# Banded attention by chunks of queries, two heads side by side on the array, and latent value products two key tiles at a time

## The chip, the cores and the metric

The kernel runs on one core of one Trainium2 chip. The metric is the device time of one execution in microseconds. The core has a matrix engine (TensorE; PE in the profile), a vector engine (VectorE, DVE), a scalar engine (ScalarE, ACT), a general engine (GpSimd, POOL) and a synchronisation engine (SyncE, SP), on whose queue nearly all transfers of this kernel are issued. Products go from SBUF into banks of PSUM, and VectorE and ScalarE read them there.

## What is computed

Two layers of a hybrid diffusion backbone over 1024 latent tokens and 256 context tokens, 1024 features wide. A layer projects the normed stream into three groups of heads (latent attention A, a state-space scan B, windowed attention C), concatenates their rows, projects them with `w_out`, and then runs a gated convolutional MLP. The part that the change touches is A and C:

```python
# A: 6 heads, 96 wide keys, 64 wide values, latent queries read context and latent keys
lc = jnp.einsum('bqhd,bkhd->bhqk', qblk, kc)
ll = jnp.einsum('bqhd,bkhd->bhqk', qblk, k)
pc, pl = joint_softmax([lc, ll])
return (jnp.einsum('bhqk,bkhd->bqhd', pc.astype(v.dtype), vc)
        + jnp.einsum('bhqk,bkhd->bqhd', pl.astype(v.dtype), v))
...
# C: 4 heads in 2 groups of keys and values, 64 wide, a band of +-128 tokens, a sink logit per head
lb = jnp.einsum('bnqgrd,bnkgd->bngrqk', qb, kb).astype(jnp.float32)
lb = jnp.where(valid[None, :, None, None], lb, NEG_INF)
lc = jnp.einsum('bnqgrd,bkgd->bngrqk', qb, kc)
ls = jnp.broadcast_to(sink.reshape(hk, r)[None, None, :, :, None, None].astype(jnp.float32),
                      lc.shape[:-1] + (1,))
_, pc, pb = joint_softmax([ls, lc, lb])
out = (jnp.einsum('bngrqk,bkgd->bnqgrd', pc.astype(v.dtype), vc)
       + jnp.einsum('bngrqk,bnkgd->bnqgrd', pb.astype(v.dtype), vb))
```

In layer 0 the context tokens attend too, to context keys alone; layer 1 leaves them out.

## The kernel before

The stream is kept feature-major, tokens along the free dimension: 1280 tokens in layer 0, 1024 in layer 1, in chunks of 512 (`CHUNKS`). TensorE runs in the order in which the code emits its instructions; the other engines are ordered by a scheduler with priorities. The foreground of a layer emits its products and calls `tick` after each group. `tick` steps generators in the background as soon as the kernel's own estimate of TensorE's time has reached the time that a generator yielded (`PACE`, 1 us for each step of C). So the order of TensorE is a weave of the foreground and of the background, and no engine chooses at run time.

In the stage between the input projections and `w_out` the foreground is A (`mla_att`), head by head: for each of ten key tiles `kt` two score chunks `s` [128 keys, 512 queries] of three products each, an exponential on ScalarE into `P` [128, 1024], the sum of the `P` tiles over key tiles into `acc` on GpSimd or VectorE, and `pv(kt - 2)`, the value product. A value product has a stationary operand of 64 columns, which fills half of the array's columns: `pv` puts queries 0 to 511 into rows 0 to 63 of the bank `py` and queries 512 to 1023 into rows 64 to 127. The rows of the queue that read x2 or x4 are such products. `finish` of the previous head follows after `kt == 2`: denominators `pd` (ones times `acc`, once more 64 columns in each half), a reciprocal of [128, 512], two multiplications. The rows `px`, `pm` and `pr` are the row maxima of the next head.

The background is B first and then C (`swa`). C runs over its four heads. For each head there are twelve score tiles `todo`: two context key tiles by two query chunks (512 queries each), then eight band tiles of at most 384 queries. Each is a product pair `s<-qq,kk` and `s<-q,k`, with mask products from `identb`, then an exponential, a sum into `acc`, and, two tiles later, `pv`, a product of 64 columns whose half of `py` is chosen by the query chunk; a band tile across position 512 is cut in two. While one head runs, `maxes(h + 1)` gives the next head's row maxima a step at a time: `sx` (context keys, two blocks of 128 queries) and `sb` (band), both over the 64 rows of one operand, read by VectorE; then `smr` on VectorE and the products `sr` that turn it into a row. At the end of a head come `pd`, with two products of one partition (`es`, the sink's exponentials) besides those of `acc`, and a reciprocal; in layer 0 a path of its own for context queries (`pc`, `rc`).

PSUM has eight banks: five with the tag "f" (A and the projections) and three with the tag "b" (all of C, with `py`, `pd`, `s`, `sx`, `sb` and `sr` among them). Weight staging (`W`) has two buffers "wst" and three each of "whi" and "wlo"; the `P` tiles of A take "whi" and "wst", the `acc` tiles of A and C take "wlo", and the first tiles of `w_out` (`w`, then `wh` on ScalarE and `wl` on VectorE) come through the same "wst".

Of the kernel before, what the change touches and what calls it, by code (L numbers as in the profile page):

```python
# [20 lines left out]
SEQ = 1024  # L21
# [4 lines left out]
BG_LAG = 1000                 # priority of background work behind the other  # L26
# [25 lines left out]
# columns of the per-layer parameter tile  # L52
# [29 lines left out]
# tensor engine time after which a step of the background work may go on, us, by layer  # L82
# [31 lines left out]
class Emit:  # L114
    def __init__(self, ctx, tc, I, out):
# [3 lines left out]
        self.t = 0.0        # estimated time of the tensor engine's queue, us  # L119
        self.bgs = []       # background work: [generator, time at which it may go on]  # L120
# [8 lines left out]
    # ------------------------------------------------ order of the tensor engine  # L129
# [76 lines left out]
    # ---------------------------------------------------------------- setup  # L206
    def setup(self):
# [12 lines left out]
        # [k, q]: 0 where the entry counts, else a large negative number  # L220
# [5 lines left out]
        # window masks [q, k]: the block before keeps k >= q, the block after keeps k <= q  # L226
# [25 lines left out]
    def tri(self, t, d):  # L252
        """[k, q]: 1 where q >= k (d = 0) or q <= k (d = 1), else 0"""
# [32 lines left out]
    # ------------------------------------------------------------- modulation  # L286
# [14 lines left out]
    def mods(self, l, ns, wtile, ahead, gap, etile=None):  # L301
        """columns 512 n .. of the modulation of layer l, feature-major in modT [128, 6 parts, 2 streams, 8]"""
# [31 lines left out]
    def mods_v(self, l, ns, wtile, gap, atile=None):  # L334
        """the same with the products on the vector engine"""
# [43 lines left out]
    def scale_ab(self, l, which, hf):  # L379
        """a = g * (1 + scale) per stream, half of the features; the shift is read from modT."""  # L380
# [17 lines left out]
    def diag(self, out, r, nb):  # L398
        """token-major columns r [128, nb] as nb diagonal blocks; ones times them is the row r on every partition"""
# [4 lines left out]
    # --------------------------------------------------------------- weights  # L404
    def wload(self, srcs, shape, stage=None, pool=False, tile=None):
        """srcs: list of (slice of the tile, AP); returns the high and the low part"""
# [5 lines left out]
        if shape[-1] == 64:  # L412
            # few columns: both parts side by side
# [14 lines left out]
    def wnext(self, n=1, ahead=3):  # L428
        """the next n weight tiles of the stream; those after them are fetched ahead"""
# [5 lines left out]
    def prod(self, w, x, psum, tok, ks=None):  # L435
        """w: (hi, lo) lists of stationary APs per k tile, x: (hi, lo) lists of moving tiles; one psum group"""
# [8 lines left out]
    def prods(self, ws, x, psums, tok):  # L445
        """several products with the same moving tiles, side by side"""
# [20 lines left out]
    def proj(self, w, x, chunks, M, put):  # L467
        """put(psum, start, end) takes each chunk of the product"""
# [6 lines left out]
    def proj2(self, wps, x, chunks, need=None):  # L475
        """wps: list of (weights, M, put)"""
# [8 lines left out]
    def cols(self, ap):  # L485
        """weight columns [1024, m] as a stream entry"""
# [3 lines left out]
    def conv(self, dst, w0, w1, w2, b):  # L490
        """centred depthwise convolution and silu; returns the consumer of the product's chunks"""
# [21 lines left out]
    def transposed(self, src, dst):  # L513
        """token blocks of src [128, NT], transposed into dst [128, NT]"""
# [9 lines left out]
    # ------------------------------------------------------------------- w_in  # L524
# [441 lines left out]
    def swa(self, l, Y):  # L966
# [49 lines left out]
        def maxes(h):  # L1016
# [5 lines left out]
            for b0 in range(0, nb, 2):  # L1022
# [6 lines left out]
                if b0 >= 8:  # L1029
                    continue  # L1030
# [935 lines left out]
```

## Time and profile before

| what | value |
|---|---|
| runs of the kernel before | 3395.48, 3403.35, 3385.51 us (median 3395.48) |
| span of the profiled execution | 3399.7 us; it has no separate time beside its span |
| TensorE busy | 3257.2 us, 96% of the span |
| VectorE, ScalarE, GpSimd busy | 1948.4, 1066.9, 784.6 us |
| the stage of the attention, layer 0 | from 504.9 us (first `sx`) to 810.1 us (first product of `w_out`) |
| the same in layer 1 | from 2300.8 to 2563.5 us |

The table is read by stage. The two stretches are 568 of 3400 us, and the change lies within them. A row of the timeline begins with the start of an instruction and its duration; products are pipelined, so what one costs the queue is the distance to the start of the next row, and a row that reads x2 joins neighbours of one shape.

### The profile page before, as it was taken

The numbers are of one execution on the slowest core, as the hardware profiler recorded it, in microseconds if no ns is written. First come the engines' busy times: TensorE is split into PE (matmuls) and PEld (weight loads), VectorE is DVE, ScalarE is ACT, GpSimd is POOL, SyncE is SP. The second block draws the span as 40 slices with busy tenths as digits, with TensorE's granted clock in tenths as the row PEclk, the third lists the DMA queues.
The fourth block names the chain that finished last, engine by engine and source line by source line (L and its number), as shares of the span: only waits on it lengthen the run. The fifth ranks groups of instructions, "written<-read, shape, count | busy, mean of one in ns | idle before, by whom it ended". The sixth has DMA issues, their size and how long they took to land.

```text
span 3399.7 us, 40235 instructions
## 1 busy us (share of the span) xinstructions
PE 3257.2 (96%) x15873; PEld 2506.1 (74%) x15873; DVE 1948.4 (57%) x2916; ACT 1066.9 (31%) x1760; POOL 784.6 (23%) x526
## 2 busy tenths in 40 slices
PE   7999879999989999999999999889999999999998
PEld 4888644446878888888888788644447788888887
DVE  5965985555376565656544644885644544344344
ACT  5344533334232111111112543543342412212222
POOL 2024443324220000000002204442442201101002
PEclk9999888999999999999999999888999999999999
DMA  7765771103122222222111445842103111111111
GB/s 258 227 184 151 246 226 40 47 1 106 38 87 81 64 89 66 87 69 81 56 38 28 145 133 150 267 149 61 40 1 112 50 44 56 50 44 50 50 50 62
DMA packets 308668, 321.63 MB, mean 95 GB/s; under 512 B 34258, under 2 KB 249187, under 8 KB 308480
## 3 DMA queue, kind: packets, MB, share of 16 engines
q1 hardware_dynamic: 307516, 318.83, 30.5%
q8 instruction: 125, 2.05, 0.2%
q0 software_dynamic: 704, 0.14, 0.1%
q14 instruction: 63, 0.52, 0.0%
q10 hardware_dynamic: 260, 0.10, 0.0%
HBM read 249.09 MB, written 68.62 MB: 93 GB/s over the span
## 4 chain that ended last, share of the span: by engine, by line
PE 85%; DVE 8%; DMA 3%; ACT 1%; issue 1%; POOL 1%; SPq 0%; DVEq 0%; POOLq 0%; ACTq 0%
PE p L142 64%; PE s L142 7%; PE py L142 6%; DMA wm<-in_w_mod_dram 1%; PE pm L142 1%; PE pd L142 1%; PE sb L142 1%; DVE mx L1300 1%; PE pn L142 1%; DVE wm L351 1%; PE pst L142 1%; DMA ab<-acsd 1%; PE ptr L147 0%; PE pt L147 0%; PE sx L142 0%
## 5 line engine op out<-in xcount | busy, mean ns | idle before, releaser
L142 PE MATMUL p<-hhi,wh 128*128 128x512 f32 (+1 forms) x2552 | 944.1, 372 | 11.2 <-DVE ft L496 5.3
L142 PE MATMUL p<-hlo,wh 128*128 128x512 f32 (+2 forms) x2552 | 941.7, 369 | 8.4 <-POOL hlo L1928 7.6
L142 PE MATMUL p<-hhi,wl 128*128 128x512 f32 (+1 forms) x2504 | 923.6, 369 | 4.9 <-DVE wl L421 3.0
L142 PEld LDWEIGHTS p<-hhi,wh 128*128 128x128 f32 x2552 | 486.3, 191 | 94.0 <-issue 6.3
L142 PEld LDWEIGHTS p<-hlo,wh 128*128 128x128 f32 (+1 forms) x2552 | 484.1, 190 | 88.2 <-POOL hlo L1928 9.4
L142 PEld LDWEIGHTS p<-hhi,wl 128*128 128x128 f32 x2504 | 476.8, 190 | 86.1 <-DVE wl L421 5.2
L1532 POOL TENSOR_TENSOR gl<-ft,gh 128x512 fp32r<-128x512 f32 (+1 forms) x110 | 153.0, 1393 | 1403.4 <-ACT gh L1531 1403.4
L1509 DVE SCALAR_TENSOR_TENSOR x<-p,modT,x 128x512 f32<-128x512 f32 (+1 forms) x480 | 327.1, 695 | 241.1 <-PE p L142 240.8
L420 ACT CAST wh<-w 128x1024 fp32r<-128x1024 f32 (+2 forms) x188 | 193.1, 1039 | 741.4 <-PE p L142 715.2
L142 PE MATMUL p<-gh,wh 128*128 128x512 f32 (+1 forms) x880 | 325.8, 370 | 1.7 <-DVE x L1509 1.5
L142 PE MATMUL p<-gl,wh 128*128 128x512 f32 (+1 forms) x880 | 324.6, 369 | 0.0
L142 PE MATMUL p<-gh,wl 128*128 128x512 f32 (+1 forms) x880 | 323.8, 368 | 0.0
L421 DVE TENSOR_TENSOR wl<-w,wh 128x1024 fp32r<-128x1024 f32 (+1 forms) x181 | 222.0, 1236 | 139.1 <-ACT wh L420 137.8
L496 DVE SCALAR_TENSOR_TENSOR ft<-p,prm,ft 128x511 f32<-128x511 f32 (+2 forms) x264 | 157.7, 612 | 175.3 <-ACT ft L500 172.5
L351 DVE SCALAR_TENSOR_TENSOR wm<-wm,mstat,wm 128x512 f32<-128x512 f32 x280 | 205.3, 776 | 55.7 <-DMA wm<-in_w_mod_dram 55.5
L1384 ACT ACTIVATE P<-s 128x512 f32<-128x512 f32 x240 | 142.6, 597 | 284.2 <-PE s L142 282.4
L142 PE MATMUL py<-P,vt 128*64 128x512 f32 (+3 forms) x728 | 224.9, 601 | 1.0 <-ACT P L1384 1.0
L1391 POOL TENSOR_TENSOR acc<-acc,P 128x1024 f32<-128x1024 f32 x69 | 167.1, 2422 | 244.3 <-ACT P L1384 241.9
L1530 DVE TENSOR_TENSOR ft<-ft,p 128x512 f32<-128x512 f32 (+1 forms) x110 | 69.4, 633 | 260.0 <-PE p L142 258.1
L142 PEld LDWEIGHTS p<-gh,wh 128*128 128x128 f32 x880 | 165.9, 189 | 30.6 <-DVE x L1509 2.0
L142 PEld LDWEIGHTS p<-gh,wl 128*128 128x128 f32 x880 | 165.6, 188 | 28.2
L142 PEld LDWEIGHTS p<-gl,wh 128*128 128x128 f32 x880 | 166.0, 189 | 27.4 <-issue 0.2
(363 smaller groups left out, 4502.8 us busy)
## 6 DMA issues: line engine op xcount, KB each, us to landing
wm<-in_w_mod_dram SPq DMA_DIRECT2D x96, 512.0 KB
w<-in_ffn_w_up_dram SPq DMA_DIRECT2D x88, 512.0 KB
w<-in_ffn_w_down_dram SPq DMA_DIRECT2D x44, 512.0 KB
w<-in_w_in_dram SPq DMA_DIRECT2D x30, 512.0 KB
ab<-acsd SPq DMA_DIRECT2D x36, 384.0 KB
tm<-tmd SPq DMA_DIRECT2D x38, 320.0 KB
xsp<-x SPq DMA_DIRECT2D x16, 640.0 KB
w<-in_w_out_dram SPq DMA_DIRECT2D x16, 512.0 KB
```

Of the source, the lines that this page charges most:

```text
L142: self.nc.tensor.matmul(out=out, lhsT=lhsT, rhs=rhs, start=start, stop=stop)
L351: nc.vector.scalar_tensor_tensor(out=acc[:, v, :], in0=w[:, i, :], scalar=c, in1=acc[:, v, :], op0=ALU.mult, op1=ALU.add)
L420: nc.scalar.copy(h, w)
L421: (nc.gpsimd if pool else nc.vector).tensor_sub(lo, w, h)
L496: nc.vector.scalar_tensor_tensor(out=dst[:, d0:d1], in0=src, scalar=w, in1=dst[:, d0:d1], op0=ALU.mult, op1=ALU.add)
L1300: nc.vector.tensor_reduce(out=m[:, j, s:s + 1], in_=p, axis=AXX, op=ALU.max)
L1384: nc.scalar.activation(P[:, q * 512:(q + 1) * 512], s, AF.Exp, scale=sc)
L1391: (nc.vector if kt in ((2, 4, 6, 8) if self.scan else (4, 7)) else nc.gpsimd).tensor_add(acc, acc, P)
L1509: self.nc.vector.scalar_tensor_tensor(out=t[:, s:e], in0=p[:, 0:e - s], scalar=self.mcol(l, v, m)[:, o:o + 1], in1=t[:, s:e], op0=ALU.mult ...
L1530: nc.vector.tensor_mul(t[:, s:e], t[:, s:e], p[:, 0:e - s])
L1532: nc.gpsimd.tensor_sub(gl[:, s:e], t[:, s:e], gh[:, s:e])
```

## The change

1. C runs over units (group of keys and values, query chunk): six in layer 0, where the context queries are a chunk of 256 and use the same code, and four in layer 1. Both heads j of the group are in one unit. Value products and denominators of head j go to rows 64j to 64j + 63, so that they come in pairs on the two halves of the array's columns. Scores are made head by head; where a tile has at most 256 queries both heads share one bank `sp`, which is kept over a yield, and one exponential reads both. The sink's `es` is added to row 64 of `acc` on GpSimd, in place of the `pd` products of one partition. One reciprocal and one multiplication by [128, 512] end a unit.
2. The maxima of C use 128 rows: `kk` holds low and high parts of the keys, `qq` the high part of the queries twice.
3. In A, the value products come two key tiles at a time, after odd `kt`, and `finish` of the previous head moves from the end of `kt == 2` to `kt == 3`, before them.
4. q is fetched for each unit and head (60 transfers instead of 24 for both layers), and the pools of C become 4 `k`, 4 `q` and 4 `P` tiles of twice the width.

The remaining lines of the difference take comments away.

```diff
-            for p in range(2):
+        units = [(kv, s, e) for kv in range(WK) for s, e in (CHUNKS if c else CHUNKS[:2])]
...
-            qb[h] = hl("qq"), hl("q1")
-            for t, r, p in ((0, 0, 0), (0, 64, 0), (1, 0, 1)):
-                nc.sync.dma_start(out=qb[h][t][r:r + 64, 0:nq].bitcast(F32), in_=self.shd[2 + j][p][rr, 0:nq])
+            qb[u] = [M.tile([128, 2, 512], F32R, tag="q", name=self.nm(x)) for x in ("qq", "q1")]
+            for j in range(2):
+                for t, r, p in ((0, 0, 0), (0, 64, 0), (1, 0, 1)):
+                    nc.sync.dma_start(out=qb[u][t][r:r + 64, j, 0:n].bitcast(F32), in_=self.shd[2 + j][p][rr, s:e])
...
-                    self.mm(out=p[:, (b - b0) * CTX:(b - b0 + 1) * CTX], lhsT=q[0:64, b * 128:(b + 1) * 128], rhs=k[0:64, CTXS],
-                            start=True, stop=True)
+                        self.mm(out=p[:, (b - b0) * CTX:(b - b0 + 1) * CTX], lhsT=q[:, j, b * 128:(b + 1) * 128], rhs=k[:, CTXS],
+                                start=True, stop=True)
...
-                    self.mm(out=p[:, 0:n], lhsT=q[0:64, b * 128:(b + 1) * 128], rhs=k[0:64, k0:k1], start=True, stop=False)
+                        self.mm(out=p[:, 0:n], lhsT=q[:, j, b * 128:(b + 1) * 128], rhs=k[:, k0:k1], start=True, stop=False)
...
-        for h in range(WH):
+        for u, (kv, s0, e0) in enumerate(units):
+            w = e0 - s0
+            mx = maxes(u + 1) if u + 1 < len(units) else iter(())
...
-                    self.mm(out=py[o:o + 64, c % 512:c % 512 + e - c], lhsT=V(k), rhs=P[:, c - c0:e - c0], start=(k == 8), stop=(k == (4 if c < 512 else 7)))
+            def pv(k, c0, c1, P, last):
+                for j in range(2):
+                    self.mm(out=py[64 * j:64 * j + 64, c0 - s0:c1 - s0], lhsT=vt[:, k * 128 + 64 * kv:k * 128 + 64 * kv + 64], rhs=P[:, j, 0:c1 - c0],
+                            start=(k == 8), stop=last)
...
+                for j in range(2):
+                    if sp is None or n > 256:
+                        sp = self.b("s")
+                    o = 256 * j if n <= 256 else 0
+                    for p, (a, b) in enumerate(((kk[0], qq[0]), (kk[1][0:65, :], qq[1][0:65]))):
+                        self.mm(out=sp[:, o:o + n], lhsT=a[:, ks], rhs=b[:, j, c0 - s0:c1 - s0], start=(p == 0), stop=(p == 1 and not masks))
+                    for t, (at, mask_) in enumerate(masks):
+                        self.mm(out=sp[:, o + at:o + at + 128], lhsT=self.identb, rhs=mask_, start=False, stop=(t == len(masks) - 1))
+                    if n > 256:
+                        nc.scalar.activation(P[:, j, 0:n], sp[:, 0:n], AF.Exp, scale=sc)
+                    elif j:
+                        nc.scalar.activation(P[:, :, 0:n], sp.rearrange("p (j n) -> p j n", j=2)[:, :, 0:n], AF.Exp, scale=sc)
+                    next(mx, None)
+                    yield PACE['swb' if j else 'swa'][l]
...
+                    nc.gpsimd.tensor_add(acc[64:65, :, 0:w], acc[64:65, :, 0:w], esr[:, :, 0:w])
...
-            for q in range(2):
-                cs = slice(q * 512, (q + 1) * 512)
-                self.mm(out=pd[64 * q:64 * q + 64, :], lhsT=self.ones[:, 0:64], rhs=acc[:, cs], start=True, stop=False)
-                self.mm(out=pd[64 * q:64 * q + 64, :], lhsT=self.ones[64:65, 0:64], rhs=esr[:, cs], start=False, stop=True)
+            for j in range(2):
+                self.mm(out=pd[64 * j:64 * j + 64, 0:w], lhsT=self.ones[:, 0:64], rhs=acc[:, j, 0:w], start=True, stop=True)
...
-                if kt > 1:
+                if kt == 3 and done:
+                    finish(*done)
+                if kt > 2 and kt % 2:
+                    pv(kt - 3)
                     pv(kt - 2)
                 next(mx, None)
-                if kt == 2 and done:
-                    finish(*done)
```

Counted along the two orders of TensorE, both layers together: the number of products stays (14808 and 14816). Runs of products with a stationary operand of 64 columns, that is stretches between two products of another kind, fall from 224 to 111. Runs of maxima over 64 rows fall from 91 to none.

On TensorE in layer 0, in the second head of A, this stood before (`py_5276` is A's value product, `s_5491` a band tile of C, `py_5262` C's value product, `sr` the row of C's maxima):

```order
L142 MATMUL py_5276<-P_5319,vt_3460 64x512 x2
L142 MATMUL pm_5488<-kh_4955,qh_4959 128x512
L142 MATMUL s_5491<-qq_4505,kk_4328 128x384
L142 MATMUL s_5491<-q_773_4506,k_727_4329 128x384
L142 LDWEIGHTS identb
L142 MATMUL s_5491<-mprev,identb 128x128
L142 LDWEIGHTS identb
L142 MATMUL s_5491<-mnext,identb 128x128
L142 MATMUL py_5262<-P_5412,vt_4321 64x384
L142 MATMUL sr_5500<-identr,smr_5270 1x128 x4
```

Around the same place stands now (`py_4804` is A's, `s_5216` a tile of C with 128 queries for each head):

```order
L142 MATMUL s_5216<-qq_4476,kk_4326 128x128
L142 MATMUL s_5216<-q_765_4477,k_727_4327 128x128
L142 LDWEIGHTS identb
L142 MATMUL s_5216<-mnext,identb 128x128
L142 MATMUL py_4804<-P_5075,vt_3460 64x512 x2
L142 MATMUL py_4804<-P_5102,vt_3460 64x512 x2
L142 MATMUL s_5216<-qq_4476,kk_4326 128x128
L142 MATMUL s_5216<-q_765_4477,k_727_4327 128x128
L142 LDWEIGHTS identb
L142 MATMUL s_5216<-mnext,identb 128x128
L142 MATMUL s_5230<-qh_4126,kh_4122 128x512
```

Two value products of A now follow each other, and the bank of `s_5216` is open from its first head's products to its second's, with A's products between.

At the end of the stage in layer 0 C came last before: its final value products, the context path and the denominators stood ahead of the first product of `w_out` (`p<-mixh,wh`).

```order
L142 MATMUL py_6198<-P_6475,vt_4321 64x256
L142 MATMUL pc_6489<-P_6484,vt_4321 64x256
L142 MATMUL pc_6489<-P_6484,ones 64x256
L142 MATMUL pc_6489<-es_4327,ones 64x256
L142 MATMUL pd_6497<-acc_6197,ones 64x512
L142 MATMUL pd_6497<-es_4327,ones 64x512
L142 MATMUL p_6545<-mixh_6205,wh_6519 128x512
```

Now the end reads:

```order
L142 MATMUL s_6491<-qh_5435,kh_5431 128x256
L142 MATMUL s_6491<-ql_5436,kh_5431 128x256
L142 MATMUL s_6491<-qh_5435,kl_5432 128x256
L142 MATMUL py_6280<-P_6458,vt_3461 64x512 x2
L142 MATMUL py_6280<-P_6475,vt_3461 64x512 x2
L142 MATMUL py_6504<-P_6492,vt_3461 64x256
L142 MATMUL py_6504<-P_6492,ones 64x256
L142 MATMUL p_6551<-mixh_6259,wh_6525 128x512
```

C's last products (`pd_6464`) stand 24 rows ahead of these now, and A's last value products come right before `w_out`; in layer 1 C ends 47 rows before it.

## Rows read from the trace of the kernel before

**Rows 1.** The page: span, engines' busy time, chain that ended last.

```profile
span 3399.7 us, 40235 instructions
...
PE 3257.2 (96%) x15873; PEld 2506.1 (74%) x15873; DVE 1948.4 (57%) x2916; ACT 1066.9 (31%) x1760; POOL 784.6 (23%) x526
...
PE 85%; DVE 8%; DMA 3%; ACT 1%; issue 1%; POOL 1%; SPq 0%; DVEq 0%; POOLq 0%; ACTq 0%
```

**Rows 2.** Windows: length; PE, PEld, DVE, ACT, POOL busy; PEclk; DMA share; GB/s.

```profile
504.90:810.10 305.20, 291.93 (x1221) 147.97 (x1221) 176.22 (x225) 112.03 (x190) 111.54 (x59) 0.94 0.15 38
2300.80:2563.50 262.70, 254.84 (x991) 121.21 (x991) 133.85 (x175) 95.33 (x161) 102.89 (x56) 0.94 0.16 40
583.00:588.00 5.00, 5.00 (x19) 2.93 (x20) 1.52 (x3) 2.69 (x6) 0.00 (x0) 0.75 0.01 2
2333.00:2360.00 27.00, 27.00 (x66) 12.69 (x65) 11.67 (x19) 5.69 (x10) 5.26 (x4) 0.50 0.00 1
```

**Rows 3.** Timeline of TensorE, 2531 to 2534 us: start, duration, instruction.

```profile
2531.39 0.40 PE L142 MATMUL s<-qh,kl 96*128 96x512 f32 x1
2531.71 1.08 PE L142 MATMUL py<-P,vt 128*64 128x512 f32 x4
2532.72 0.50 PE L142 MATMUL s<-qh,kh 97*128 97x512 f32 x1
2533.06 0.40 PE L142 MATMUL s<-ql,kh 96*128 96x512 f32 x1
2533.29 0.40 PE L142 MATMUL s<-qh,kl 96*128 96x512 f32 x1
```

**Rows 4.** Timeline of TensorE, 2548 to 2555 us: three pairs, a single product.

```profile
2548.65 2.79 PE L142 MATMUL py<-P,vt 128*64 128x512 f32 x12
2551.38 0.45 PE L142 MATMUL s<-qq,kk 128*128 128x384 f32 x1
...
2553.32 0.86 PE L142 MATMUL py<-P,vt 128*64 128x384 f32 x2
2554.11 0.44 PE L142 MATMUL s<-qq,kk 128*128 128x384 f32 x1
```

**Rows 5.** Timeline of TensorE, 2516 us: a head's denominators, two of four rows.

```profile
2516.46 1.07 PE L142 MATMUL pd<-acc,ones 128*64 128x512 f32 x2
2517.46 1.07 PE L142 MATMUL pd<-es,ones 1*64 1x512 f32 x2
```

**Rows 6.** Timeline of TensorE, 528 us: a maximum over 64 rows.

```profile
528.79 0.40 PE L142 MATMUL px<-kh,qh 96*128 96x256 f32 x2
529.11 0.44 PE L142 MATMUL sb<-k,qq 64*128 64x384 f32 x1
...
529.89 0.39 PE L142 MATMUL s<-ql,kh 96*128 96x512 f32 x1
```

**Rows 7.** Timeline of TensorE, 2332 to 2334 us: the context maxima of C.

```profile
2332.71 0.50 PE L142 MATMUL sx<-k,qq 64*128 64x256 f32 x2
2333.14 1.12 PE L142 MATMUL py<-P,vt 128*64 128x512 f32 x2
```

**Rows 8.** Lines, layer 0's stage: count, busy, mean ns, idle before and releaser.

```profile
L1335 DVE RECIPROCAL acc<-pd 128x512 f32<-128x512 f32 x5 | 16.8, 3356 | 4.1 <-PE pd L142 4.1
...
L1337 DVE TENSOR_TENSOR ya<-py,acc 64x512 f32<-64x512 f32 x10 | 6.9, 686 | 0.1
```

**Rows 9.** Timeline of TensorE, 582 us: behind a wait, idle in brackets.

```profile
582.06 1.01 PE L142 MATMUL sr<-identr,smr 128*1 128x128 f32 x8 [2.88 <-DVE smr L1043]
582.87 0.73 PE L142 MATMUL s<-qh,kh 97*128 97x512 f32 x1
```

**Rows 10.** Timeline, 799 to 804 us: A's last product, weights of w_out.

```profile
799.91 0.38 PE L142 MATMUL py<-P,vt 128*64 128x256 f32 x1
...
802.03 1.16 DVE L421 TENSOR_TENSOR wl<-w,wh 128x1024 fp32r<-128x1024 f32 x1
```

**Rows 11.** Timeline, 2554 us: weights of w_out in layer 1.

```profile
2554.57 1.23 DVE L421 TENSOR_TENSOR wl<-w,wh 128x1024 fp32r<-128x1024 f32 x1 [1.15 <-ACT wh L420]
```

More of the change, by code (lines that the diff above doesn't have):

```diff
@@ L1047, in maxes @@
                 p = self.b("sr")
-                for b in range(b0, b1):
-                    self.mm(out=p[0:1, (b - b0) * 128:(b - b0 + 1) * 128], lhsT=mr[:, b:b + 1], rhs=self.identr, start=True, stop=True)
-                nc.scalar.copy(q1[64:65, b0 * 128:b1 * 128], p[0:1, 0:(b1 - b0) * 128])
+                for b in range(nb):
+                    self.mm(out=p[0:1, b * 128:(b + 1) * 128], lhsT=mr[:, j, b:b + 1], rhs=self.identr, start=True, stop=True)
+                nc.scalar.copy(q1[64:65, j, 0:nb * 128], p[0:1, 0:nb * 128])
@@ L1101, in swa @@
                 next(mx, None)
-                yield PACE['swa'][l]
-                next(mx, None)
-                yield PACE['swb'][l]
-            if c:
-                s = self.b("s")
-                for t in range(2):
-                    ks = slice(SEQ + t * 128, SEQ + (t + 1) * 128)
-                    for p, (a, b) in enumerate(terms):
-                        self.mm(out=s[:, t * 256:(t + 1) * 256], lhsT=a[:, ks], rhs=b[:, CTXS], start=(p == 0), stop=(p == 1))
-                Pc = M.tile([128, 512], F32, tag="P", name=self.nm("P"))
-                nc.scalar.activation(Pc, s, AF.Exp, scale=sc)
@@ L1113, in swa @@
             for a in queue:
                 pv(*a)
-                yield PACE['swv'][l]
+            yield PACE['swv'][l]
             for _ in mx:
                 yield PACE['swx'][l]
-            if h + 2 < WH:
-                load(h + 2)
-            if c:
-                rc = M.tile([128, 512], F32, tag="P", name=self.nm("rc"))
-                pc = self.b("pc")
-                for t in range(2):
-                    self.mm(out=pc[0:64, 0:256], lhsT=V(8 + t), rhs=Pc[:, t * 256:(t + 1) * 256], start=(t == 0), stop=(t == 1))
-                    self.mm(out=pc[64:128, 0:256], lhsT=self.ones[:, 0:64], rhs=Pc[:, t * 256:(t + 1) * 256], start=(t == 0), stop=False)
-                self.mm(out=pc[64:128, 0:256], lhsT=self.ones[64:65, 0:64], rhs=esr[:, CTXS], start=False, stop=True)
-                nc.vector.reciprocal(rc[0:64, 0:256], pc[64:128, 0:256])
-                nc.vector.tensor_tensor(out=yc[kv][rows, CTXS], in0=pc[0:64, 0:256], in1=rc[0:64, 0:256], op=ALU.mult)
@@ L1129, in swa @@
-            pd = self.b("pd")
-            for q in range(2):
-                cs = slice(q * 512, (q + 1) * 512)
-                self.mm(out=pd[64 * q:64 * q + 64, :], lhsT=self.ones[:, 0:64], rhs=acc[:, cs], start=True, stop=False)
-                self.mm(out=pd[64 * q:64 * q + 64, :], lhsT=self.ones[64:65, 0:64], rhs=esr[:, cs], start=False, stop=True)
-            rc = acc[:, 0:512]
-            nc.vector.reciprocal(rc, pd)
-            for q in range(2):
-                nc.vector.tensor_tensor(out=yc[kv][rows, q * 512:(q + 1) * 512], in0=py[64 * q:64 * q + 64, :], in1=rc[64 * q:64 * q + 64, :],
-                                        op=ALU.mult)
+            if u + 2 < len(units):
+                load(u + 2)
@@ L1139, in swa @@
+            pd = self.b("pd")
+            for j in range(2):
+                self.mm(out=pd[64 * j:64 * j + 64, 0:w], lhsT=self.ones[:, 0:64], rhs=acc[:, j, 0:w], start=True, stop=True)
+            rc = acc[:, 0, 0:w]
+            nc.vector.reciprocal(rc, pd[:, 0:w])
+            nc.vector.tensor_tensor(out=yc[kv][:, s0:e0], in0=py[:, 0:w], in1=rc, op=ALU.mult)
             yield PACE['swe'][l]
```

123 lines of the change are left out of this document (57 added, 66 removed).

## The prediction, before the changed kernel ran

> **What bounds the kernel now.** I read the page first: TensorE is busy for 3257 of 3400 us, and 85% of the chain that ended last are its instructions [rows 1]. So work taken from its queue shows, as long as nothing else takes its place. Then the windows of the two stages that the change touches [rows 2]: in layer 0 TensorE is busy for 291.93 of 305.20 us, in layer 1 for 254.84 of 262.70, which leaves 13.3 and 7.9 us of idle time. VectorE is busy for 176.22 and 133.85 us, 55% of both stages together, GpSimd for about 37%, ScalarE for 37%. The reader is to see that TensorE is the bound by the mean, and that no other engine is close. The last view is TensorE's timeline, because "busy" does not say at what rate the array works: there I read the distance from one start to the next.
>
> **What a run of 64-column products costs.** A score product of 512 queries takes 0.23 us of queue (2533.06 to 2533.29). Around one pair of value products the distances are 0.32 before, 1.01 for the pair, and 0.34 for the score behind it [rows 3]. Three pairs take 2.73 us from start to start [rows 4], so each pair after the first takes (2.73 - 1.01)/2 = 0.86. A run therefore costs 0.09 + 0.15 + 0.11 = 0.35 us beyond its columns. A single product of 384 queries takes 0.79 us [rows 4]; 384/512 of 0.86 is 0.645, and 0.15 remains: a product alone costs what a pair costs, and half of the array is empty beside it. The same holds for the denominators of C: four products of a head, 1.00 us apart each [rows 5].
>
> **The change, term by term.** (1) Columns. At 0.86 us per 512 columns, the value products of a head of C are 4 times 512 context and 2816 band columns, less 256 where the two parts of a cut tile go side by side: 4608 columns, 7.7 us. A unit has 2 times 512 and 1408 columns for both heads: 4.1 us. With 8 heads before and 8 latent units after: -29 us. Denominators: 4 products, 3.44 us, against one pair, 0.86 us, eight times: -20.6. In layer 0 the context path had five columns of 256 per head (twice values, twice ones, and the sink), 2.1 us if none pair up and 1.3 with the pairs; the two context units need 1.3 each, about -2.6 in all. Together -52.
>
> (2) Runs. 224 before, 111 after; 113 times 0.35 is -39.6. Most come from C's pairs and from A's `pv`, which halves its runs. A's products themselves stay.
>
> (3) Maxima over 64 rows. From the start of the `px` row to that of `s<-ql,kh` in layer 0 are 1.10 us [rows 6]. Two `px` of 256 columns, `sb` of 384, two masks and one `s` at the rate of 0.23 per 512 are 0.23 + 0.17 + 0.11 + 0.23 = 0.74, so up to 0.36 is extra, some of it the masks' own start. In layer 1 two `sx` take 0.43 up to the next row instead of 0.23 [rows 7], 0.20 extra, where the switch out is shared with a value product. Over 128 rows both become ordinary products. I take 0.27, the middle, since the 91 runs are of both kinds: -24.6 (ends -18 and -33).
>
> The sum on TensorE is -52 - 39.6 - 24.6 = **-116 us**.
>
> (4) Waits for banks. C lives in three banks, and VectorE reads and frees them in its order; a block of denominators is a reciprocal of 3.36 us and two multiplications of 0.69 [rows 8], 4.7 us in which no maximum is read. One such wait is at 582 us, 2.88 us behind `smr` [rows 9]. VectorE's work stays nearly the same, so with the stages 100 us shorter its share rises from 310/568 = 0.55 to 310/470 = 0.66. If idle time grows like share/(1 - share), from 1.2 to 1.9, the 21 us of idle become 33: +12 (ends 0, since a shorter `pd` also frees a bank earlier, and +30). In layer 0 there are five rounds of `smr` and `sr` under the units instead of three under the heads, which is inside that.
>
> The Trainium skill, page TensorEngine Tiling (Array Packing), Performance Considerations under PSUM Bottleneck, speaks against the change here: tiling speeds up TensorE but not the evacuation of PSUM, which may then become the bottleneck. By the rows VectorE's share does not get there in the mean, and the sum keeps +12; by the rule it would lose far more, which is the second rival.
>
> (5) The end of the stage. C closed the stage before, and the first weights of `w_out` came in behind it: `wl` ends at 803.19 in layer 0, after A's last product had started at 799.91 [rows 10], and at 2555.80 in layer 1 [rows 11], while A's products had ended at 2551.38 [rows 4]. Now A closes the stage, and the staging buffer still comes free with `pv(7)`, at `kt == 9` as before. So about 3.0 and 4.4 us are uncovered, +7. Behind the wait at 582 the granted clock was 0.75 over five microseconds [rows 2], and `s` took 0.73 instead of 0.50 [rows 9]; two such stretches are another +3. Together +10 (ends 0 and +15).
>
> (6) At nothing. The sink's addition on GpSimd comes at the second tile of a unit, three or more tiles ahead of `pd`, and GpSimd is idle for 194 and 160 us of the stages [rows 2]: 6 and 4 additions would have to take some 30 us each to fill that. The 36 further transfers are issued a unit ahead, about 45 us before use; six issues per unit would have to take 7 us each. `finish` one key tile later holds a head's `acc` longer, and two tiles of A now take the very buffer of the head before, so their first addition on GpSimd waits for `finish`; TensorE does not need the sum before its own `pd`. Without that cover it would be some 5 us twice, inside the end of (4).
>
> Sum: -116 + 12 + 10 = **-94 us**. The profiled span of 3399.7 is 4 us above the median of the runs, 3395.48, so the forecast is 3395 - 94, near **3301 us**. With the ends of (3), (4) and (5) it is -65 to -125: 3270 to 3330.
>
> **Rivals.** *The clock comes back too.* The granted clock has two levels, 2.4 and 1.2 GHz; a mean of 0.94 over the stages is 12% of 568 us at the lower, 68 us. From 2333 to 2360 it was 0.50 while TensorE was busy without a gap, on maxima over 64 rows and half-empty value products [rows 2]. If these stretches are gone with what stood in them, half of 68 us comes back on top: 3267, or 3246 to 3275 with what the other ends allow. Against it: other low stretches follow idle time, which grows.
>
> *Evacuation gives half back.* This is the skill's rule as a mechanism here: in stretches where VectorE holds the banks, TensorE saves nothing but waits longer. If half of the 116 goes into such waits, -58 + 10 = -48: 3347, or 3335 to 3378. For it speaks the wait behind `smr`; against it VectorE's 55%.
>
> *Nothing moves.* The columns saved would have to lie beside something else that ends the stage. Against it: 21 us of idle in 568.
>
> *Slower.* The shared score bank `sp` is open over a yield, so with `py` only one bank of three is left for maxima and `pd`. There are 28 such tiles (24 band tiles of at most 256 queries and 4 of context). If each waited for a block of VectorE, 4.7 us, that is +133 against -94: 3434. It decides from 94/28 = 3.4 us each. Against it: the block comes once a unit, not with each tile.
>
> **Chances.** Forecast 0.60, clock 0.13, evacuation 0.15, nothing 0.08, slower 0.04. About 0.5% is what a measurement of this kernel tells from no change (its three runs span 3385.5 to 3403.4). The first three are faster by more than that: 0.88. The range from 3258 to 3355 holds the forecast's own 3270 to 3330, most of the clock's case and half of the evacuation's.
>
> **What would show it.** Right: the two stages near 255 and 217 us with TensorE's idle near 15 us each; `py` rows of A as x8 with 1.87 us up to the next row; `pd` of C one pair; `sb` followed at the plain rate; the product of `w_out` behind `wl`. Wrong: idle of 30 us and more in a stage, released by VectorE's reads of maxima; waits of `s` for a bank ahead of tiles with 256 queries; a mean clock below 0.9; or, the other way, a clock of 1.00 through layer 1's stage.

## The result, and the profile after

The changed kernel took 3342.82 us (median of four runs, 3339.44 to 3349.32), beside 3392.44 of the kernel before on the same chip (four runs): a ratio of 0.985, 95% interval 0.983 to 0.988. So it is faster by about 50 us, in the direction of the forecast, at little more than half of its 94 us. It lies inside the whole range (3258 to 3355), but outside the 3270 to 3330 that the forecast's own terms allowed: the range reached that far only to take in the rival of the evacuation. The profiled execution was the slowest of the four, with a span of 3347.6 us.

The page of the changed kernel, its span, busy times and chain, against [rows 1]:

```profile
span 3347.6 us, 40209 instructions
...
PE 3160.3 (94%) x15857; PEld 2496.6 (75%) x15857; DVE 1948.8 (58%) x2912; ACT 1068.7 (32%) x1764; POOL 804.2 (24%) x518
...
PE 72%; DVE 8%; DMA 2%; issue 1%; ACT 1%; POOL 1%; SPq 0%; DVEq 0%; POOLq 0%; ACTq 0%
```

TensorE is busy for 97 us less, and its share of the chain fell from 85 to 72%: waits came in. The windows of the two stages say where, each again from the first `sx` to the first product of `w_out`, columns as in [rows 2]:

```profile
511.40:783.10 271.70, 243.09 (x1220) 139.94 (x1219) 183.83 (x229) 112.67 (x194) 130.04 (x59) 0.95 0.20 56
2280.40:2504.00 223.60, 206.36 (x980) 115.47 (x979) 137.59 (x177) 92.26 (x156) 107.46 (x49) 0.94 0.15 44
```

In layer 0 the stage went from 305.2 to 271.7 us, in layer 1 from 262.7 to 223.6, together -72.6 us. TensorE's busy time fell by 97.3 (546.8 to 449.5), and its idle time (length less busy) rose by 24.7: from 13.3 to 28.6 us in layer 0 and from 7.9 to 17.2 in layer 1. The rest of the program took 20.5 us back. From the start to the first `sx` it is 511.4 instead of 504.9 us; between the stages 1497.3 instead of 1490.7; behind the second stage 843.6 instead of 836.2. Nearly all of these 20.5 are idle time of TensorE: 11.1, 6.4 and 2.4 us more in the three stretches. Part is scatter: the same start took between 504 and 511 us in the profiles of this study, and of their fourteen the one before has the least idle time outside the stages, the one after the most ahead of the first `sx`.

**The queue itself** reads as forecast. TensorE's timeline of the changed kernel, to be held against [rows 3] and [rows 6]:

```profile
2320.22 0.33 PE L142 MATMUL sb<-kk,qq 128*128 128x384 f32 x1
2320.39 0.23 PE L142 MATMUL sb<-mprev,identb 128*128 128x128 bf16 x1
...
2322.87 0.48 PE L142 MATMUL sx<-kk,qq 128*128 128x256 f32 x2
2323.28 1.94 PE L142 MATMUL py<-P,vt 128*64 128x512 f32 x8
2325.14 0.40 PE L142 MATMUL pr<-identr,mr 128*1 128x128 f32 x4
```

Two value products of A are one run now and take 1.86 us up to the next start (2323.28 to 2325.14); the prediction had 1.87. A maximum `sb` of 384 queries over 128 rows takes 0.17 us up to its mask, the plain rate.

**The idle time** has three large places in the two profiles. The largest is in layer 0. TensorE's timeline at the end of a unit of C, and then VectorE's and GpSimd's over the same stretch:

```profile
747.62 1.98 PE L142 MATMUL pd<-acc,ones 128*64 128x512 f32 x4 [10.38 <-POOL acc L1112]
```

```profile
729.35 1.49 DVE L733 TENSOR_TENSOR mixl<-yb,mixh 128x1280 fp32r<-128x1280 f32 x1 [0.59 <-ACT mixh L732]
733.79 5.34 DVE L733 TENSOR_TENSOR mixl<-yb,mixh 128x1280 fp32r<-128x1280 f32 x1 [2.94 <-ACT mixh L732]
739.05 3.62 DVE L733 TENSOR_TENSOR mixl<-ya,mixh 128x1280 fp32r<-128x1280 f32 x1
742.60 3.63 DVE L1112 TENSOR_TENSOR acc<-acc,P 128x768 f32<-128x768 f32 x1
```

```profile
716.55 2.38 POOL L1109 TENSOR_TENSOR acc<-P,P 128x1024 f32<-128x1024 f32 x1 [6.33 <-ACT P L1101]
...
721.33 2.37 POOL L1110 TENSOR_TENSOR acc<-acc,es 1x1024 f32<-1x1024 f32 x1
...
732.50 2.96 POOL L733 TENSOR_TENSOR mixl<-yb,mixh 128x1280 fp32r<-128x1280 f32 x1
735.41 2.37 POOL L1380 TENSOR_TENSOR acc<-P,P 128x1024 f32<-128x1024 f32 x1
737.86 3.47 POOL L1382 TENSOR_TENSOR acc<-acc,P 128x1024 f32<-128x1024 f32 x1
741.29 4.12 POOL L733 TENSOR_TENSOR mixl<-ya,mixh 128x1280 fp32r<-128x1280 f32 x1
746.31 1.26 POOL L1112 TENSOR_TENSOR acc<-acc,P 128x512 f32<-128x512 f32 x1 [0.90 <-DVE acc L1112]
```

`pd` stands in TensorE's queue and waits 10.38 us for the last sum of its unit, the GpSimd addition that starts at 746.31. Read upwards: that addition continues the one on VectorE at 742.60, which stands behind two splits `mixl`; they belong to `w_out`'s operands and are emitted where A's last head starts. GpSimd has a split of its own at 741.29, and two sums of A before it. TensorE could have gone on with A's scores, but its order puts `pd` first.

The second place is the end of the stages: the first products of `w_out`, with the release of each in brackets.

```profile
783.07 0.80 PE L142 MATMUL p<-mixh,wh 128*128 128x512 f32 x1 [4.94 <-ACT wh L420]
...
784.50 0.79 PE L142 MATMUL p<-mixh,wl 128*128 128x512 f32 x1 [0.21 <-DVE wl L421]
...
2503.99 0.50 PE L142 MATMUL p<-mixh,wh 128*128 128x512 f32 x1 [3.21 <-ACT wh L420]
...
2505.25 0.79 PE L142 MATMUL p<-mixh,wl 128*128 128x512 f32 x1 [0.39 <-DVE wl L421]
```

```profile
781.97 1.04 ACT L420 CAST wh<-w 128x1024 fp32r<-128x1024 f32 x1 [3.49 <-DMA w<-in_w_out_dram]
```

They wait for `wh`, 4.94 and 3.21 us, and ScalarE's `wh` in turn for the transfer of the weights (last row). The product at the wait in layer 0, and the one some 1.3 us behind it in both layers, take 0.79 or 0.80 us instead of 0.50, the lower clock; in layer 1 the product at the wait still takes 0.50. The third place is ahead of C's first maximum in layer 0, where one wait of 5.9 us for a maximum of A is new; the 5.3 us for `mr` behind it was 5.5 before:

```profile
480.96 0.80 PE L142 MATMUL pm<-kh,qh 96*128 96x512 f32 x1 [5.93 <-DVE mx L1291]
...
488.77 0.58 PE L142 MATMUL pr<-identr,mr 128*1 128x128 f32 x4 [5.31 <-DVE sink L993]
```

### The profile page after: what moved, and what is told of

The parts are those of the page before. It is cut to its first block, busy times and chain, and to the rows that moved or that the text cites. A ratio compares the mean times of both kernels' runs of the same rounds, so it can differ in the third digit from the quotient of the medians.

```text
span 3347.6 us, 40209 instructions
## 1 busy us (share of the span) xinstructions
PE 3160.3 (94%) x15857; PEld 2496.6 (75%) x15857; DVE 1948.8 (58%) x2912; ACT 1068.7 (32%) x1764; POOL 804.2 (24%) x518
## 4 chain that ended last, share of the span: by engine, by line
PE 72%; DVE 8%; DMA 2%; issue 1%; ACT 1%; POOL 1%; SPq 0%; DVEq 0%; POOLq 0%; ACTq 0%
PE p L142 58%; PE s L142 5%; PE py L142 4%; DVE mx L1291 1%; DMA wm<-in_w_mod_dram 1%; DVE wm L351 1%; PE pm L142 1%; PE pn L142 1%; PE pd L142 1%; DVE acc L1326 1%; PE sb L142 0%; DMA ab<-acsd 0%; DVE sh L725 0%; DVE smx L1045 0%; PE pst L142 0%
## 5 line engine op out<-in xcount | busy, mean ns | idle before, releaser
L1375 ACT ACTIVATE P<-s 128x512 f32<-128x512 f32 x240 | 142.5, 598 | 247.0 <-PE s L142 240.8
L142 PE MATMUL py<-P,vt 128*64 128x512 f32 (+3 forms) x744 | 172.3, 578 | 0.0
```

The source lines that it names most:

```text
L142: self.nc.tensor.matmul(out=out, lhsT=lhsT, rhs=rhs, start=start, stop=stop)
L1375: nc.scalar.activation(P[:, q * 512:(q + 1) * 512], s, AF.Exp, scale=sc)
```

## The experiments

Each kernel was timed against the kernel before on the same chip; ratios are to that kernel. Where an experiment starts from the changed kernel, its ratio is to be held against 0.985 (0.983 to 0.988).

**A's value products alone.** The kernel before with this part of the change:

```diff
-                if kt > 1:
+                if kt == 3 and done:
+                    finish(*done)
+                if kt > 2 and kt % 2:
+                    pv(kt - 3)
                     pv(kt - 2)
                 next(mx, None)
-                if kt == 2 and done:
-                    finish(*done)
```

> The kernel before with one part of the change: A's value products two key tiles at a time and finish at kt == 3. It removes 43 of the 100 or so runs of 64-column products that the whole change removes. Theory of the prediction (0.35 us a run, nothing lost): about -15 us, ratio 0.9955. Rival (what later finish and later value products cost in idle time, as seen in the changed kernel before its first maximum of C, eats it): within 3 us of before, ratio 0.999 to 1.001.

Measured: 3378.04 us against 3395.99, ratio 0.995 (0.993 to 0.997), 16 us, which agrees with the price. The profiled pair does not show it as cleanly: by its rows (the table in the next section) the products are 9 us shorter, and more of its difference is the clock.

**The maxima over 128 rows alone.** The kernel before with

```diff
-            (q, q1), k = qb[h], kb[h // 2][1]
+            (q, q1), k = qb[h], kb[h // 2][0]
...
-                    self.mm(out=p[:, (b - b0) * CTX:(b - b0 + 1) * CTX], lhsT=q[0:64, b * 128:(b + 1) * 128], rhs=k[0:64, CTXS],
+                    self.mm(out=p[:, (b - b0) * CTX:(b - b0 + 1) * CTX], lhsT=q[:, b * 128:(b + 1) * 128], rhs=k[:, CTXS],
```

and the same for `sb`.

> The kernel before with C's maxima over 128 rows and nothing else. Price in the prediction, 0.27 us for each of 91 runs: -25 us, ratio 0.993. By the distances in the changed kernel's trace (maxima 12 us shorter): -12 us, ratio 0.9965. If VectorE's reading bounds the maxima: 0.

Measured: 3375.35 us, ratio 0.995 (0.993 to 0.997), 18 us. Between the two prices. The windows of its two stages:

```profile
505.10:795.70 290.60, 277.16 (x1221) 145.00 (x1221) 174.39 (x225) 111.99 (x190) 111.65 (x59) 0.95 0.16 40
2287.00:2528.80 241.80, 233.52 (x990) 115.75 (x990) 131.68 (x175) 94.57 (x159) 103.64 (x56) 0.99 0.16 41
```

Busy time is 36 us below [rows 2], but part of it is the clock: 0.99 in layer 1 instead of 0.94. Counting 2 times (1 - clock) of the length as time at the lower level, the stages had 68 us of it before and 34 here, worth 17 us, which leaves 19 for the products; counted row by row it is 19 for the clock and 17 for the products, 0.19 us for each of 91 runs where the prediction took 0.27. This profile is of one of the faster of six runs (3371 us); over all of them the mean clock is 0.974, and 0.973 in the kernel before.

**The change without A's part.** The changed kernel with the first experiment's edit undone.

> The changed kernel with A's value products one key tile at a time again and finish at kt == 2. It has 48 more runs of 64-column products. By 0.35 us a run: 17 us above the changed kernel, near 3360 and ratio 0.990 to before. If the two-tile products lose in waits what they save: equal to the changed kernel, ratio 0.985, or below it.

Measured: 3339.46 us, ratio 0.984 (0.982 to 0.986). So in time A's part, worth 16 us alone, is worth nothing beside C's units. Row by row (the table in the next section) its saving is there all the same: the changed kernel's products are 16.4 us shorter than this one's, 0.34 for each of 48 runs. More time at the lower clock (15.8 us) and more idle time (9.2 us) take that back in the profiled pair. The mean clock of the runs is 0.971 to 0.974 here and 0.967 to 0.971 in the changed kernel. C's units, by subtraction, give 55 - 18 = 37 us in time, where columns and 52 runs at 0.35 us made 70; row by row their products are 57 us shorter. `pd` waits here too, in the context unit of layer 0, and for the sink's addition (L1110) this time:

```profile
751.19 1.12 PE L142 MATMUL pd<-acc,ones 128*64 128x256 f32 x4 [11.66 <-POOL acc L1110]
```

**The splits later.** The changed kernel with

```diff
-            if h == NH - 1:
-                last()
...
+                if kt == 8 and h == NH - 1:
+                    last()
```

> The changed kernel with the five splits of Y for w_out (last()) emitted at kt == 8 of the last head of A instead of at its start. Theory: in layer 0 these splits stood on VectorE and GpSimd ahead of the last sums of a unit of C, and TensorE waited 10.4 us for them at pd; without them there the wait falls to 1 us or less, 8 to 9 us off the time, ratio to before 0.983. Rival: the splits then come later than w_out needs them, and the same time is lost in front of its first products; ratio 0.985 as the changed kernel, or higher.

Measured: 3345.54 us, ratio 0.986 (0.984 to 0.988). The rival was right. `pd` waits 3.92 us instead of 10.38, but `w_out` waits 5.26 us in layer 0 and 6.18 in layer 1 (4.94 and 3.21 in the changed kernel), each time with ScalarE's `wh` waiting for the transfer of the weights. What delays the transfer there was not followed further.

**The first weights of `w_out` early.** The changed kernel; at the start of A's last head two tiles are fetched into other buffers, and they are split ahead of `pv(8)`:

```diff
             if h == NH - 1:
                 last()
+                fetch()
...
+            if h == NH - 1:
+                split()
             pv(NCH - 2)
```

> The changed kernel with the first two weight tiles of w_out fetched into other buffers at the start of A's last head and split before its pv(8). Theory: w_out's first products waited 4.9 and 3.2 us for weights and then ran some 7 and 3 us at the lower clock, about 13 us in all; with the weights there the time falls by 8 to 13 us, ratio to before 0.982. Rival: the wait only moves to the next thing that is late (the splits of Y, ScalarE's queue), ratio 0.985 as the changed kernel.

Measured: 3331.69 us, ratio 0.981 (0.978 to 0.984), some 13 us below the changed kernel by the ratios, whose intervals overlap a little (0.983 to 0.984). In TensorE's timeline the first product of `w_out` has no wait ahead of it, in either layer, and runs at the upper clock. Layer 0:

```profile
770.12 0.38 PE L142 MATMUL py<-P,vt 128*64 128x256 f32 x1
...
770.43 0.50 PE L142 MATMUL p<-mixh,wh 128*128 128x512 f32 x1
770.77 0.39 PE L142 MATMUL p<-mixl,wh 128*128 128x512 f32 x1
```

`pd` still waits 10.15 us.

**The sink on TensorE.** The changed kernel without the addition on GpSimd, and

```diff
+            for j in range(2):
+                self.mm(out=pd[64 * j:64 * j + 64, 0:w], lhsT=self.ones[64:65, 0:64], rhs=esr[:, j, 0:w], start=False, stop=True)
```

> The changed kernel with the sink's exponentials added by products of one partition in pd again, a pair per unit, and no addition on GpSimd. If the addition was hidden, as the prediction had it: 10 more pairs of 0.86 to 1.0 us and nothing else, 9 to 10 us slower than the changed kernel, ratio to before 0.988. If the ten additions of 2.4 us delay the sums that pd waits for: that loss comes back, ratio 0.984 to 0.986 or below.

Measured: 3337.83 us, ratio 0.983 (0.980 to 0.986). It was expected 9 us slower if the additions were hidden, and is not slower; by the middle of the intervals it is 8 us faster, which the intervals do not separate from no change. The wait of 10 us is gone: the longest wait of a `pd` in layer 0 is 1.18 us. The stage of layer 0 is no shorter for it in this profile (271.1 us): it has 12.6 us less idle time, 3 us more products, and loses 9 us more to the lower clock.

**The denominators later.** The changed kernel with a yield after each of the last three value products, and

```diff
             for a in queue:
                 pv(*a)
-            yield PACE['swv'][l]
+                yield PACE['swv'][l]
+            yield 3.0
```

> The changed kernel with the denominators of a unit later: a yield after each of the last three value products, as in the kernel before, and one of 3 us before pd. Theory: pd follows the last sum too closely, and TensorE's waits for it (13 us in layer 0, 10.4 of them once) go: 8 to 12 us faster, ratio to before 0.982. Rival: sums and reads of C are only later as a whole, since they queue behind A's on GpSimd and VectorE, and the wait stays: ratio 0.985.

Measured: 3344.23 us, ratio 0.985 (0.982 to 0.988), and `pd` still waits 8.03 us, for VectorE's sum. Moving `pd` by some microseconds does not help, because the sums of C are held up as a whole.

**`finish` at `kt == 2`.** The changed kernel with `finish` where it was, the value products still in twos.

```diff
-                if kt == 3 and done:
+                if kt == 2 and done:
```

> The changed kernel with finish at kt == 2 as before, the value products still two key tiles at a time. Without A's two-tile products the changed kernel lost nothing (ratio 0.984), though alone they gave 16 us. If the later finish (its accumulator is waited for on GpSimd, its reciprocal comes later) is what costs: 5 to 10 us faster than the changed kernel, ratio 0.983. If the two-tile products themselves cost, by reaching the sums and maxima of C sooner: as the changed kernel or slower, by 11 more runs at 0.3 us, 0.985 to 0.987.

Measured: 3325.32 us, ratio 0.979 (0.977 to 0.982): 20 us below the changed kernel, from one line. The windows of its stages, and the longest wait of a `pd` in layer 0:

```profile
506.90:762.60 255.70, 238.78 (x1219) 136.16 (x1219) 180.93 (x227) 112.75 (x194) 129.75 (x59) 0.98 0.21 58
2257.60:2483.20 225.60, 205.62 (x979) 111.47 (x979) 142.28 (x177) 91.56 (x156) 107.27 (x50) 0.96 0.20 55
```

```profile
746.45 1.12 PE L142 MATMUL pd<-acc,ones 128*64 128x256 f32 x4 [2.87 <-POOL acc L1110]
```

Against the changed kernel, layer 0's stage is 16 us shorter. Idle time is 16.9 us instead of 28.6, and TensorE's busy time 4.3 us shorter, with the clock at 0.98 instead of 0.95. In layer 1 the stage is 2 us longer. Over the whole execution 18 of the 21 us between the two profiles are the clock, 11 are idle time, and the products, with 11 more runs, are 8 us longer. The clock is on record for every run: 0.975 to 0.977 in the five of this kernel, 0.967 to 0.971 in the four of the changed kernel.

**`finish` at `kt == 2` without the units.** The first experiment with this line.

> The kernel before with A's value products two key tiles at a time, but finish at kt == 2. If the later finish costs by itself what it cost in the changed kernel (20 us): near 3360, ratio 0.990. If it costs only where it meets C's units (their sums, pd and A's splits in the last head): as with finish at kt == 3, ratio 0.995 to 0.996.

Measured: 3378.37 us, ratio 0.995 (0.993 to 0.997), as with `finish` at `kt == 3`. So a later `finish` costs nothing that shows by itself; it costs where it meets C's units.

**The splits one head earlier.** The changed kernel with

```diff
-            if h == NH - 1:
-                last()
...
+                if kt == 5 and h == NH - 2:
+                    last()
```

> The changed kernel with the five splits of Y emitted one head earlier (at kt == 5 of the head before A's last). Theory: the 10.4 us wait of pd in layer 0 was a meeting of a unit's last sums with these splits on VectorE and GpSimd; apart from each other the wait falls below 3 us and w_out is no later, 8 to 15 us with the clock, ratio to before 0.981 to 0.983. Rival: another pair of things meets, and the time stays within 4 us of the changed kernel, 0.984 to 0.987.

Measured: 3339.76 us, ratio 0.984 (0.981 to 0.986). The wait is gone, as TensorE's timeline at that `pd` shows, and `w_out` waits as in the changed kernel:

```profile
740.69 1.08 PE L142 MATMUL pd<-acc,ones 128*64 128x512 f32 x4 [0.72 <-POOL acc L1112]
...
773.59 0.77 PE L142 MATMUL p<-mixh,wh 128*128 128x512 f32 x1 [5.14 <-ACT wh L420]
```

Layer 0's stage is 266.3 us long, 5.4 less, and has 22.5 us of idle time instead of 28.6. The time is 5 us below the changed kernel by the ratios, which the intervals don't separate from no change. The mechanism is shown, its worth is smaller than expected: of the 9.7 us that this wait lost, 6.1 are left as less idle time, and the rest turned up as other waits. The one wait is thus not the bulk of what the forecast missed.

**Both repairs, and both with the sink on TensorE.** The changed kernel with `finish` at `kt == 2` and the early weights; then with the sink in `pd` as well.

> The changed kernel with finish at kt == 2 and the first two weight tiles of w_out fetched early. If the two losses are separate (20 and 13 us): near 3312, ratio 0.9755. If both stood for the same wait in layer 0: as with finish at kt == 2 alone, 0.979.

> As the one before, with the sink's exponentials added by TensorE in pd. If the additions on GpSimd cost in themselves: 4 to 8 us less, ratio 0.973. If they cost only by the wait in layer 0 that finish at kt == 2 has mostly removed: 5 to 9 us more, for ten more pairs of products, ratio 0.977 to 0.978.

Measured: 3321.84 us, ratio 0.978 (0.976 to 0.981), and 3323.06 us, ratio 0.979 (0.976 to 0.981). Both beat the changed kernel, by 22 to 24 us by the ratios, and the kernel before by 72 to 74, but not the single line of `finish` by more than the intervals. By the middles the gains of the early weights (13 us) and of `finish` (20 us) come to 24 together, not 33, and with both in, moving the sink's addition changes nothing that can be measured.

## Why the prediction was right in sign and twice too large

**The balance.** The time of a profiled execution can be split row by row. The distance from one start to the next, less the idle time in it, is what a product costs the queue. This, times the granted clock, is what the product would cost at the upper level. The rest is what the lower level added, and idle time. Worked out so from the traces, in us:

| kernel | span | products at the upper clock | added by the lower clock | idle |
|---|---|---|---|---|
| before | 3399.7 | 3165.8 | 91.4 | 142.5 |
| changed | 3347.6 | 3076.3 | 84.0 | 187.2 |
| A's value products alone | 3373.9 | 3156.6 | 66.9 | 150.4 |
| maxima over 128 rows alone | 3369.6 | 3150.1 | 64.7 | 154.8 |
| the change without A's part | 3338.9 | 3092.7 | 68.2 | 178.0 |
| `finish` at `kt == 2` | 3326.5 | 3084.3 | 65.9 | 176.3 |

Stretches with the same code differ by up to 5 us in the third column, and the last two columns scatter more, so only the larger differences count. From before to after, products give 89.5 us where the forecast had 116. Idle time and clock together take back 37 where it had 22 (12 for waits, 10 for the end of the stage). So 26 of the 42 us that are missing in this pair are products that were never saved, and 15 are waits and clock beyond those forecast.

**TensorE is the bound, and work taken from its queue shows.** Right: the two stages are 72.6 us shorter, and the two parts that could be tried alone were worth 16 and 18 us.

**Columns and runs (-52, -39.6).** Right in kind, too large by some 15 us. The rows of value products are 39.5 us shorter, those of the denominators 24.5, the context path's own 6.4, and the products beside them about 7. The price of a run came out at 0.34 where A's part is added to C's units, and at 0.21 (by products) to 0.37 (by time) where it is alone. The number of runs was too large: by the rows of the traces, of which some can be missing, they fall from 214 to 114, 100 where 113 were counted along the orders, which is 4.6 us of the term. The columns were not measured apart.

**Maxima over 64 rows (-24.6).** Right in kind, too large: the price of 0.27 was taken between 0.20 and 0.36, and alone it was 0.19, about 17 us in the products and 18 in time. In the changed kernel the rows of the maxima are 12 us shorter.

**The sum of -116, the term that was mis-sized.** It measured 89.5 us, most of it in the stages (85) and some 6 ahead of the first `sx`, where A's two-tile products have already begun. About ten of the 26 us are the maxima's, the others lie with columns and runs. Why a run costs 0.34 in one place and less in another was not tried.

**Waits (+12), right in size by luck, and wrong in mechanism.** The prediction sized the idle time by VectorE's share and three banks. VectorE's share did rise as worked out, to 321/495 = 0.65 where 0.66 was expected, and bank waits stayed small: the longest ahead of a maximum or a score of C in these stages is 1.7 us. Idle time rose by 24.7 us in the stages, of which 8.2 are `w_out`'s, a term of its own; the 16.5 left are near the forecast, but they are another wait. What came was `pd` waiting for sums: 10.4 us once in layer 0, and some 13 with the shorter ones there. The sentence that failed is "TensorE does not need the sum before its own `pd`", said of A's sums: it does need C's right there, and C's sums queue behind A's, behind the sink's additions and behind the splits. Removing the splits from that place, or the additions, took the wait away; moving `pd` by some microseconds did not. But each removal was worth 5 to 8 us by the middles, which the intervals do not tell from none, so this wait is not what makes the forecast twice too large.

**The sink's addition "at nothing".** Wrong in this weave: GpSimd has the time in the mean (idle for 142 of 271.7 us), but not in the order. Without it the changed kernel is at least no slower, with ten more pairs of products. Whether it costs anything once the long wait is gone is not shown: without it, both repairs took 1 us more, where a free addition would have meant 5 to 9 us more, and the intervals are wider than that.

**`finish` "at nothing".** Wrong by 20 us beside C's units; the cover that failed is not `finish`'s own time, since without C's units it costs nothing that shows. What is shown is that with `finish` at `kt == 2` the long wait of that `pd` is gone and the clock is higher in every run. In the profiled pair 18 of 21 us are this clock. Which of the orders on VectorE and GpSimd `finish` shifts, and what in them moves the clock, was not isolated: one change of the weave moves every later meeting, and the change without A's part, with `finish` at `kt == 2`, had a wait of 11.66 us again.

**The end of the stage (+10).** Right, a little small: the waits were 4.94 and 3.21 us (3.0 and 4.4 expected), and taking them away was worth 13 us.

**Outside the stages (0).** Not forecast: 20.5 us in the profiled pair, 19.9 of them idle time. About 3 of the 20.5 is what the new wait of 5.9 us ahead of C in layer 0 leaves over after A's two-tile products have saved their part there; nine of the ten other profiles with these products have a wait of 5.9 us at that place, and none without them has. Some 4 is scatter of the start. Between the stages idle time ranges from 43.7 to 55.6 us over the profiles, without order by what was changed (45.7 before, 52.1 now). Behind the second stage the lower clock added 5 us more than before.

**The rivals.** The time is that of the rival in which evacuation gives half back (3347), but its mechanism did not happen: no bank held TensorE for long. By the rule of the Trainium skill (TensorEngine Tiling (Array Packing), PSUM Bottleneck) the evacuation may become the bottleneck; the page names a speedup of TensorE by four for it, far from the one here. In this case's trace it did not, with VectorE at 0.65 and waits for banks under 2 us. What grew was the wait for sums, between engines that are all far from full. The clock did not come back with the change: 54 us of the stages at the lower level instead of 68, and over the whole execution 218 instead of 213. In the profiles of each part alone it did in layer 1 (0.98 and 0.99), but over all their runs the mean clock is 0.972 and 0.974, against 0.973 before. The shared bank `sp` cost nothing that can be seen.

**The signs.** Of those named for being right, the rows came as written: `py` as x8 with 1.86 us, `pd` of C one pair, `sb` at the plain rate. `w_out` waits for `wh` first and for `wl` (0.21 and 0.39 us) behind it. The stages did not come out: 271.7 us with 28.6 idle where 255 with 15 were expected, and 223.6 with 17.2 where 217 with 15 were. Layer 0's idle time is just short of the 30 us named as a sign of being wrong, and its longest wait was for a sum and not for reads of maxima.

## What to carry to other kernels

When TensorE's order is fixed, a product that needs a sum of the same unit is a rendezvous: before pricing it at nothing, list what stands ahead of the last sum on each engine that adds to it, and what is emitted there from other parts of the program. Gains of single parts need not add: A's part and C's units together gave what C's units gave alone, and undoing a side effect of A's part, one line, was worth more (20 us) than A's part alone (16). Split the time into products, idle time and clock before calling a part worthless: A's 16 us of products were there, and were lost to the other two. Work that closed a stage also covered the loads of the next; where it goes, fetch those loads earlier.

## What the runs showed of the hardware

An addition on GpSimd took the same time on one partition as on 128 where the row is as long. In layer 0's stage of the change without A's part, the sink's addition of 1x1024 and the sum of 128x1024 took 2.37 us each:

```profile
L1109 POOL TENSOR_TENSOR acc<-P,P 128x1024 f32<-128x1024 f32 x4 | 9.5, 2368 | 13.7 <-ACT P L1101 7.2 <-DVE smr L1050 6.5
L1110 POOL TENSOR_TENSOR acc<-acc,es 1x1024 f32<-1x1024 f32 x4 | 9.5, 2368 | 0.3
```

In the changed kernel that holds for six of the sink's eight additions of 1x1024 (2.35 to 2.38 us); two took 3.23 and 3.41, and the two of 1x512 took 2.27 and 2.12 where 128x512 took 1.27. What held these up was not followed.

VectorE's split of 128x1280 took 1.49 us at 729.35, and 5.34 and 3.62 us at 733.79 and 739.05, where GpSimd's instructions beside it took up to 4.12 us (above). Beside the short one GpSimd was the slower: its addition of 128x768 at 729.79 took 2.76 us, the seven others of that shape 1.81 to 1.84. What slows them was not tried. And the stretch behind a wait can cost as well: from 739.80, inside the wait of 10.38 us, to 753.40 the granted clock was 0.50, the lower level:

```profile
739.80:753.40 13.60, 5.78 (x14) 2.52 (x16) 10.08 (x4) 1.19 (x2) 7.04 (x4) 0.50 0.00 0
```

From 747.62, where TensorE goes on, to 753.4 these are 5.8 us of work at half speed. The clock tells runs of one kernel apart too: the kernel before took 3382.53 us in the run with a mean clock of 0.975 and 3413.49 in the one with 0.967, the fastest and the slowest of its runs.
